# Low parts of twelve weight blocks by accumulating DMAs in a one-core hybrid layer

## The chip, the core and the metric

The kernel runs on one core of a Trainium2 chip. The core's engines work side by side, each through its own list of instructions in order: TensorE (PE, matmuls and transpositions), VectorE (DVE), ScalarE (ACT), GpSimd (POOL) and SyncE (SP, which issues transfers). The metric is the device time of one launch in microseconds. The kernel before takes 933.18 us in the median of three runs (931.96 to 933.34).

## The reference

One layer of a model in fp32 for 512 prompt rows and 64 sample rows (576 columns in all once transposed), width 1024:

```python
h = x + concat[gdn(n), diff_attention(n)] @ w_out          # n = rmsnorm(x) @ w_in, split
h = h + mem_attn(rmsnorm(h), mem_k, mem_v, w_mem_q, w_mem_o)
h = h + square(relu(rmsnorm(h) @ w_ff1)) @ w_ff2
y = rmsnorm(h)
```

The outputs are y for both groups, the new keys and values, the recurrent states and the memory keys and values. The change concerns three products with a 1024 x 1024 weight: `w_out`, `w_mem_q` and `w_mem_o`.

## The kernel before, in words

**Three products for one.** Every fp32 product is made of three fast products in the type fp32r, which rounds its operand. A value v is kept as a high part hi = round(v) and a low part lo = v - hi, and the kernel adds hi x hi, hi x lo and lo x hi in PSUM.

**A weight block** is 128 columns of a weight, all 1024 rows: a tile of 128 partitions by 8 x 128 values, 512 KB. `split_weights` makes its parts. SP loads `raw` (L569; rows of 128 values, 512 bytes); ACT casts it into the high part `wh` (L573); DVE writes the low part `wl` = raw - wh (L574). There are three buffers for `raw`, two for `wh` and two for `wl`, so a cast can start only when PE has left the high part of the block before the last one.

**A block's product.** `project` (L581) multiplies a block with the transposed activations in two halves of 256 and 320 columns, each into its own PSUM bank, over eight steps of 128 rows. In the half of 256 the two products that use `wh` are one matmul of 512 columns, followed by one of 256 with `wl`; in the half of 320 there are two with `wh` and one with `wl`. A block so has 40 matmuls. The activation's high and low parts stand in the tiles `u`.

**The stages that the change touches**, in the order of time: the output projection with eight blocks m = 0 to 7 (356.5 to 407.4 us); the memory query, four heads with two blocks each, eight blocks, with the attention of each head behind them (407.4 to 487.8 us); the memory output with eight blocks in the order m = 0, 4, 1, 5, 2, 6, 3, 7 (487.8 to 547.3 us). In the memory output `combine(m)` normalises the columns of the residual, and between the last blocks the first matmuls of the feed-forward part (FFN) are started.

**What sets the order.** The instructions are traced, and then a planner in the same file puts each engine's list into a fixed order. A `Step` holds one instruction with a modelled duration (L94 on; for a transfer a rate in bytes per ns and a lead in ns). `Arrangement.run` plays the lists out with these costs (`execute`, L392), `improve` tries priorities and keeps the order with the shortest modelled end, and `arrange` fixes that order by dependences. In this model a transfer holds its engine for 530 ns, its bytes go one after another over one wire, and a margin `SPARE` of 2500 ns is added to its landing. The order of PE's list is thus made from modelled times, while each instruction waits on the chip for its real inputs. POOL issues no transfer in this kernel; between 356 and 547 us its list holds a single operation, the power -1/2 of the query's norm (`rpow`, L618).

Of the kernel before, what the change touches and what calls it, by code (L numbers as in the profile page):

```python
# [9 lines left out]
F32 = mybir.dt.float32  # L10
F32R = mybir.dt.float32r
AF = mybir.ActivationFunctionType
ALU = mybir.AluOpType
# [3 lines left out]
P = 128  # L17
D = 1024
KT = 8
# [22 lines left out]
COLD = 9000.0  # L42
BACKLOG = 2500.0
SPARE = 2500.0
# [49 lines left out]
class Step:  # L94
# [24 lines left out]
    def cost(self):  # L119
        on_chip = [a.size for a in self.ins + self.outs if a.on_chip]  # L120
        n = max(on_chip + [1])
        wide = [a for a in self.ins if a.size > 1 or len(self.ins) == 1]
        bank = any(a.bank for a in wide)
        column = any(a.size == 1 for a in self.ins)
        if self.engine == "PE":
            x, w = self.ins
            self.passes = 2 if "32r" not in str(self.inst.ins[0].dtype) and not self.turn else 1
            self.fetch = 111.0 if self.turn else max(105.0 * w.size / 128, 55.0)
            n = x.size * self.passes
            by_size = {512: 229.0, 384: 175.0, 320: 146.5, 288: 132.5, 256: 119.0}  # L130
            single = self.passes == 1 and n > 128
            self.step = single and by_size.get(n) or max(0.42 * n + (12 if single else 4), 56.0)
            latency = {512: 400, 384: 340, 320: 310, 288: 295, 256: 281, 128: 276, 64: 222}
            self.time = latency.get(n) or (222 + 0.418 * n if n < 128 else 172 + 0.43 * n)
        elif self.is_dma:
            self.bytes = 4 * self.outs[0].size * self.outs[0].dims[0][1]
            row = 4 * min(self.ins[0].run, self.outs[0].run)
            self.rate = 270.0 if row <= 512 else 300.0 if row < 2048 else 320.0 if row < 4096 else 380.0
            if row >= 1024 and min(a.dims[0][1] for a in self.ins + self.outs if a.on_chip) <= 64:
                self.rate *= 0.6  # L140
            self.lead = 1600.0 if self.ins[0].on_chip else 1950.0
        elif self.engine == "ACT":
            self.time = (155 if bank else 190) + 0.84 * n + 100 * (len(self.ins) > 1) + 60 * (len(self.outs) > 1)
        elif self.engine == "DVE":
            if self.op == "Memset":
                self.time = 60 + 0.83 * n
            elif self.op == "Reciprocal":
                self.time = 165 + 5.4 * n
            elif self.op == "TensorScalarPtr" and len(wide) == 1:
                rate = 0.53 if not any(a.bank for a in wide) else 1.16 if n > 300 else 1.04  # L150
                self.time = 150 + rate * n + 60 * (column and n < 300)
            else:
                self.time = 145 + 1.06 * n + 62 * (column and self.op == "TensorScalarPtr")
        else:
            power = self.op == "TensorTensor" and any(a.tile.startswith("nhalf") for a in self.ins)
            by_op = dict(TensorTensor=(185, 2.2), TensorScalarPtr=(185, 2.2), TensorScalarAffineSelect=(150, 1.8))
            base, rate = (500, 140) if power and n <= 16 else by_op.get(self.op, (100, 0.85))
            self.time = base + rate * n


class Arrangement:
# [230 lines left out]
    def execute(self, s):  # L392
        at = self.start(s)
        if s.boundary:
            return at
        if s.engine == "PE":
            for i in range(s.passes):
                began, step = self.last
                slow = 2 if began < COLD else 1
                at = max(began + slow * step, max(began, 0 if i else s.ready) + slow * max(s.fetch, self.least))  # L400
                self.last, self.least = (at, s.step), 0.0
            self.least = 112.0 if s.turn else 0.0
            return at + s.time + 14
        if s.is_dma:
            self.clock[s.engine] = at + 530
            self.wire = max(at + s.lead, self.wire) + s.bytes / s.rate
            return self.wire + (SPARE if at > 2 * COLD else 0.0)
        if s.engine == "ACT":
            table = dict(Silu="Silu", Exp="Exp").get(str(getattr(s.inst, "func", "")).split(".")[-1])
            if table not in (None, self.table):  # L410
                self.table = table
                at += 1300
        self.clock[s.engine] = at + s.time - OVERLAP[s.engine]
        if s.port:
            self.held[s.engine] = at + s.time
        return at + s.time + 10
# [15 lines left out]
def hybrid_layer_kernel(  # L432
# [10 lines left out]
    V, A, G = nc.vector, nc.scalar, nc.gpsimd  # L443
# [120 lines left out]
        nc.sync.dma_start(raw, w[:, c0 : c0 + P].rearrange("(k p) n -> p k n", p=P))  # L564
        return raw

    def split_weights(w, shape):
        raw = wp.tile(shape, F32, tag="raw", name=nm("raw"), bufs=3)
        nc.sync.dma_start(raw, w.rearrange("(k p) n -> p k n", p=P))  # L569
        wh = wp.tile(shape, F32R, tag="wh", name=nm("wh"))  # L570
        wl = wp.tile(shape, F32R, tag="wl", name=nm("wl"))
        with tc.high_priority():
            A.copy(wh, raw)  # L573
            V.tensor_tensor(wl, raw, wh.bitcast(F32), ALU.subtract)  # L574
        return wh, wl

    def weights(w, c0, kt=KT):

        return split_weights(w[:, c0 : c0 + P], [P, kt, P])

    def project(w, x, evac, kt=KT, halves=HALVES, merge=True):  # L581

# [287 lines left out]
    G_Q, G_FF, G_FIN = 16, 24, 32  # L870
# [83 lines left out]
    for typ in (1, 0, 2):  # L954
# [5 lines left out]
        for h in range(H):  # L960
            m = typ * 4 + h
# [7 lines left out]
            n = SOFF + DEC  # L969
# [77 lines left out]
    with after(behind_keys[1]):  # L1047
        for lb, e in enumerate(near_):
            s = 2 << lb
# [321 lines left out]
    oa = pair(2, F32R)  # L1371
# [247 lines left out]
    for w, out in ((w_mem_k, o_mk), (w_mem_v, o_mv)):  # L1619
        dst = tokens  # L1620
        for f in range(2):
# [23 lines left out]
            if out is o_mv and f == 0:  # L1645
                ob = pair(5, F32R)
# [50 lines left out]

    hx = [pair(i, F32R) for i in (4, 3)]
    for m in range(KT):
        project(weights(w_out[0], m * P), (oa, ob), add_residual(m, True, hx, G_Q))  # L1700
    cols = norm_columns()
    accs[0] = None

# [21 lines left out]
    mo = []  # L1725
    for h in range(H):
        qh = [small("kd" if h % 2 else "aT", [P, T], dt=F32R) for i in range(2)]
        ql = cp.tile([P, 2, T], F32R, tag=f"qz{h % 2}", name=nm("ql"))
        for i in range(2):
            def split_query(b, a0, n, more=None):  # L1730
                if more is not None:
                    q = small("zr", [P, 320])[:, :n]
                    add_to(q, b, more)
                    b = q
                A.copy(qh[i][:, a0 : a0 + n], b)
                V.tensor_tensor(ql[:, i, a0 : a0 + n], b, qh[i][:, a0 : a0 + n].bitcast(F32), ALU.subtract)

            project(weights(w_mem_q[0], (2 * h + i) * P), hx, split_query)

        pT = [lows(*tags) for tags in ((("p1", "p1"), ("S", "vn")) if h % 2 else (("vb", "vb"), ("KQ", "KQ")))]  # L1740
        pS = small("an", [P, 2, DEC])
        for t, (q0, _) in enumerate(QT):
            t0, n = TT[t]
            kk, kl = (mkT, mkl) if t < 4 else (cmT, cml)
            b = bank(("gs", "g0", "g1")[t % 3])
            for i in range(2):
                m, q = 2 * h + i, slice(q0, q0 + P)
# [7 lines left out]
            p = small("p0", [P, 512])  # L1755
# [15 lines left out]
        for i in range(2):  # L1771
            b, b2 = bank(("g0", "gs")[i]), bank(("g1", "ba")[i])
            fs = slice((2 * h + i) * P, (2 * h + i + 1) * P)
            for bi in range(2):
                m = 2 * h + i
# [159 lines left out]
        halves_to(*ws[4], A22)  # L1935

    for i, m in enumerate((0, 4, 1, 5, 2, 6, 3, 7)):
        project(weights(w_mem_o[0], m * P), mo, add_residual(m, False))
        combine(m)
        if i == 3:  # L1940
            load_stage(0)
            split_first()
# [328 lines left out]
```

## Time and profile before

| | us |
|---|---|
| median of three runs | 933.18 (931.96 to 933.34) |
| profiled execution | 931.63 |
| its span in the trace | 929.9 |
| PE busy | 920.5 (99%) |
| DVE busy | 743.5 (80%) |
| ACT busy | 586.4 (63%) |
| POOL busy | 98.2 (11%) |

The span is the time from the first to the last record of the trace; 1.7 us of the execution lie outside it. In a timeline row the first number is the start in us from the span's beginning, the second the duration, then engine, line, operation, output and inputs by the program's names without their numbers, and in brackets the idle time of the engine before it and what ended that. A group of instructions has its count behind the x, then busy time and the mean in ns of one. Matmuls overlap: the time between two starts, and not the duration in the row, is what one costs PE. In the rows of stretches each engine stands with busy us and the count of instructions, then the granted clock of PE, the share of time in which the sixteen DMA engines were busy, and what they moved.

### The profile page before, as it was taken

How to read it: one execution, taken by the hardware profiler on the slowest of the kernel's cores; microseconds unless marked ns; L12 is line 12 of the kernel's file. 1: busy time of each engine (PE TensorE's matmuls, PEld its weight loads, DVE VectorE, ACT ScalarE, POOL GpSimd, SP SyncE). 2: the span in 40 equal slices, each digit the busy share in tenths (PEclk: the TensorE clock that was granted, in tenths of full speed). 3: DMA queues.
4: the chain of work that ended last, by engine and by line, in shares of the span. 5: the costliest groups of instructions: out<-in, count | busy, mean ns of one | idle time of the engine just before them, and what ended most of it. 6: DMA issues, size and time to landing. Idle time of an engine off the chain costs nothing.

```text
span 929.9 us, 17536 instructions
## 1 busy us (share of the span) xinstructions
PE 920.5 (99%) x6648; PEld 891.9 (96%) x6648; DVE 743.5 (80%) x1622; ACT 586.4 (63%) x1333; POOL 98.2 (11%) x192
## 2 busy tenths in 40 slices
PE   9999999999999999999999999999999999999997
PEld 8999999999999888999999999999999999999996
DVE  6888897887777776666567889699999588999954
ACT  6664886545566674445445567677778577877654
POOL 2452111110100000000000000021100021200001
PEclk9999999999999999999999999999999999999999
DMA  7823421127444755331212322322323222233202
GB/s 208 270 55 91 116 58 29 35 69 196 118 118 133 266 190 173 91 118 49 62 46 76 95 68 81 92 91 91 91 92 124 82 68 91 92 101 126 85 8 103
DMA packets 111727, 96.45 MB, mean 104 GB/s; under 512 B 6584, under 2 KB 98970, under 8 KB 111130
## 3 DMA queue, kind: packets, MB, share of 16 engines
q1 hardware_dynamic: 111354, 94.80, 34.5%
q8 instruction: 52, 0.85, 0.4%
q10 hardware_dynamic: 288, 0.52, 0.2%
q14 instruction: 33, 0.27, 0.1%
HBM read 80.32 MB, written 9.75 MB: 97 GB/s over the span
## 4 chain that ended last, share of the span: by engine, by line
PE 96%; issue 1%; ACT 1%; DMA 0%; DVE 0%; POOL 0%; DVEq 0%; POOLq 0%; SPq 0%
PE pr L530 61%; PE g L530 12%; PE ba L530 12%; PE gs L530 7%; PE ba L534 3%; PE g L534 2%; DMA u<-in_x_prompt_dram 0%; PE gs L534 0%; ACT u L793 0%; POOL tiny L618 0%; DVEq L2267 0%; DVE w L1807 0%; DVE raw L1902 0%; ACT w L1806 0%; POOLq L2267 0%
## 5 line engine op out<-in xcount | busy, mean ns | idle before, releaser
L530 PE MATMUL pr<-u,wh 128*128 128x320 f32 (+3 forms) x1536 | 351.5, 318 | 0.8 <-ACT u L793 0.4
L530 PEld LDWEIGHTS pr<-u,wh 128*128 128x128 f32 x1536 | 252.2, 190 | 9.8 <-ACT wh L726 0.6
L530 PE MATMUL pr<-u,wl 128*128 128x256 f32 (+2 forms) x912 | 244.9, 301 | 0.0
L530 PEld LDWEIGHTS pr<-u,wl 128*128 128x128 f32 x912 | 163.8, 189 | 1.4 <-ACT Dt L1193 0.2
L574 DVE TENSOR_TENSOR wl<-raw,wh 128x1024 fp32r<-128x1024 f32 x65 | 79.5, 1223 | 30.7 <-ACT wh L573 29.4
L573 ACT CAST wh<-raw 128x1024 fp32r<-128x1024 f32 x65 | 68.2, 1049 | 56.3 <-PE pr L530 45.6
L530 PE MATMUL pr<-x,w 128*128 128x288 f32 x432 | 66.3, 294 | 0.0
L1807 DVE TENSOR_TENSOR w<-raw,w 128x512 fp32r<-128x512 f32 x83 | 57.2, 711 | 7.2 <-PE pr L530 4.3
L530 PEld LDWEIGHTS pr<-x,w 128*128 128x128 f32 x432 | 60.3, 188 | 0.0
L530 PE MATMUL pr<-x,wl 128*128 128x288 f32 x384 | 57.5, 296 | 0.1
L530 PEld LDWEIGHTS pr<-x,wl 128*128 128x128 f32 x384 | 52.9, 188 | 0.6 <-ACT pr L2073 0.4
L530 PE MATMUL ba<-u,wl 128*128 128x288 f32 x360 | 52.7, 295 | 0.2 <-ACT gs L2009 0.2
L1806 ACT CAST w<-raw 128x512 fp32r<-128x512 f32 x83 | 49.0, 619 | 3.1 <-DVE raw L1902 1.0
L530 PEld LDWEIGHTS ba<-u,wl 128*128 128x128 f32 x360 | 49.3, 188 | 0.4 <-ACT gs L2009 0.4
L2078 DVE TENSOR_TENSOR u<-u,pr 128x288 f32<-128x288 f32 x84 | 37.5, 450 | 8.6 <-PE pr L530 7.3
L1807 DVE TENSOR_TENSOR wl<-raw,wl 128x512 fp32r<-128x512 f32 x58 | 39.1, 700 | 5.2 <-ACT wl L1806 4.5
L2076 ACT COPY u<-pr 128x288 f32<-128x288 f32 x76 | 30.2, 397 | 20.7 <-PE pr L530 20.1
L530 PE MATMUL pr<-wh,u 128*128 128x512 f32 x128 | 41.9, 400 | 0.0
L1664 DVE TENSOR_TENSOR u<-u,pr 128x256 f32<-128x256 f32 (+1 forms) x48 | 21.8, 454 | 22.8 <-PE pr L530 21.6
L2056 POOL TENSOR_TENSOR keep<-x 128x288 f32<-128x288 f32 x8 | 6.8, 847 | 309.7 <-DVE x L2030 309.7
L1806 ACT CAST wl<-raw 128x512 fp32r<-128x512 f32 x58 | 33.4, 620 | 6.4 <-DVE raw L1899 4.4
L618 POOL TENSOR_TENSOR tiny<-tiny,nhalf 128x1 f32<-128x1 f32 (+1 forms) x13 | 8.9, 694 | 206.5 <-DVE tiny L2163 98.3
(542 smaller groups left out, 2073.0 us busy)
## 6 DMA issues: line engine op xcount, KB each, us to landing
raw<-in_w_ff_dram SPq DMA_DIRECT2D x48, 512.0 KB
raw<-in_w_in_dram SPq DMA_DIRECT2D x27, 512.0 KB
raw<-in_w_ff_dram SPq DMA_DIRECT2D x32, 256.0 KB
raw<-in_w_mem_k_dram SPq DMA_DIRECT2D x8, 512.0 KB
raw<-in_w_mem_v_dram SPq DMA_DIRECT2D x8, 512.0 KB
raw<-in_w_out_dram SPq DMA_DIRECT2D x8, 512.0 KB
raw<-in_w_mem_q_dram SPq DMA_DIRECT2D x8, 512.0 KB
raw<-in_w_mem_o_dram SPq DMA_DIRECT2D x8, 512.0 KB
```

The costliest lines, as they stand in the source:

```text
L530: nc.tensor.matmul(out, lhsT, rhs, start=start, stop=stop, skip_group_check=skip_group_check)
L534: nc.tensor.transpose(out, in_, ident[:n, :n])
L573: A.copy(wh, raw)
L574: V.tensor_tensor(wl, raw, wh.bitcast(F32), ALU.subtract)
L618: G.tensor_tensor(out, in_, bc(nhalf[: in_.shape[0], 0:1], list(in_.shape)), ALU.pow)
L1664: V.tensor_tensor(hm, hm, b, ALU.add)
L1806: A.copy(hi, src)
L1807: V.tensor_tensor(lo, src, hi.bitcast(F32), ALU.subtract)
L2056: G.tensor_tensor(t, q[:, 3], q[:, 1], ALU.subtract)
L2076: A.copy(to, b[:, :n])
L2078: V.tensor_tensor(to, to, b[:, :n], ALU.add)
```

## The change

`split_weights` gets an argument `by`. With `by="add"` ACT casts the high part as before, ACT then writes its negative into `wl`, and a transfer issued by POOL adds `raw` onto it, from one on-chip tile to the other. With `by="cast"` the high part, too, is written by a transfer of POOL that casts. With `by="again"` ACT casts and negates, and four transfers of POOL add the block's rows onto `wl` straight from DRAM, two of the eight steps each. Twelve blocks take these ways: `w_out` m = 1, 3, 5, 7 the first, the second block of each head's query the second, and `w_mem_o` m = 4, 5, 6, 7 the third. The planner gets figures of its own for POOL's transfers. Lines 569 to 581 and later move by 2 to 14 in the changed kernel.

```diff
--- before.py
+++ after.py
@@ -139,6 +139,8 @@
             if row >= 1024 and min(a.dims[0][1] for a in self.ins + self.outs if a.on_chip) <= 64:
                 self.rate *= 0.6
             self.lead = 1600.0 if self.ins[0].on_chip else 1950.0
+            if self.engine == "POOL":
+                self.rate, self.lead = 250.0, 2000.0
         elif self.engine == "ACT":
             self.time = (155 if bank else 190) + 0.84 * n + 100 * (len(self.ins) > 1) + 60 * (len(self.outs) > 1)
         elif self.engine == "DVE":
@@ -402,9 +404,9 @@
             self.least = 112.0 if s.turn else 0.0
             return at + s.time + 14
         if s.is_dma:
-            self.clock[s.engine] = at + 530
+            self.clock[s.engine] = at + (1000 if s.engine == "POOL" else 530)
             self.wire = max(at + s.lead, self.wire) + s.bytes / s.rate
-            return self.wire + (SPARE if at > 2 * COLD else 0.0)
+            return self.wire + (SPARE if at > 2 * COLD and s.engine != "POOL" else 0.0)
         if s.engine == "ACT":
             table = dict(Silu="Silu", Exp="Exp").get(str(getattr(s.inst, "func", "")).split(".")[-1])
             if table not in (None, self.table):
@@ -564,19 +566,31 @@
         nc.sync.dma_start(raw, w[:, c0 : c0 + P].rearrange("(k p) n -> p k n", p=P))
         return raw
 
-    def split_weights(w, shape):
+    def split_weights(w, shape, by=None):
         raw = wp.tile(shape, F32, tag="raw", name=nm("raw"), bufs=3)
         nc.sync.dma_start(raw, w.rearrange("(k p) n -> p k n", p=P))
         wh = wp.tile(shape, F32R, tag="wh", name=nm("wh"))
         wl = wp.tile(shape, F32R, tag="wl", name=nm("wl"))
         with tc.high_priority():
-            A.copy(wh, raw)
-            V.tensor_tensor(wl, raw, wh.bitcast(F32), ALU.subtract)
+            if by == "cast":
+                G.dma_start(wh, raw)
+            else:
+                A.copy(wh, raw)
+            if by is None:
+                V.tensor_tensor(wl, raw, wh.bitcast(F32), ALU.subtract)
+            else:
+                A.activation(wl, wh.bitcast(F32), AF.Identity, scale=-1.0)
+                if by == "again":
+                    for k in range(0, 8, 2):
+                        src = w[k * P : (k + 2) * P, :].rearrange("(k p) n -> p k n", p=P)
+                        G.dma_start(wl[:, k : k + 2], src, accum_op=ALU.add)
+                else:
+                    G.dma_start(wl, raw, accum_op=ALU.add)
         return wh, wl
 
-    def weights(w, c0, kt=KT):
-
-        return split_weights(w[:, c0 : c0 + P], [P, kt, P])
+    def weights(w, c0, kt=KT, by=None):
+
+        return split_weights(w[:, c0 : c0 + P], [P, kt, P], by)
 
     def project(w, x, evac, kt=KT, halves=HALVES, merge=True):
 
@@ -1697,7 +1711,7 @@
 
     hx = [pair(i, F32R) for i in (4, 3)]
     for m in range(KT):
-        project(weights(w_out[0], m * P), (oa, ob), add_residual(m, True, hx, G_Q))
+        project(weights(w_out[0], m * P, by="add" if m % 2 else None), (oa, ob), add_residual(m, True, hx, G_Q))
     cols = norm_columns()
     accs[0] = None
 
@@ -1735,7 +1749,7 @@
                 A.copy(qh[i][:, a0 : a0 + n], b)
                 V.tensor_tensor(ql[:, i, a0 : a0 + n], b, qh[i][:, a0 : a0 + n].bitcast(F32), ALU.subtract)
 
-            project(weights(w_mem_q[0], (2 * h + i) * P), hx, split_query)
+            project(weights(w_mem_q[0], (2 * h + i) * P, by="cast" if i else None), hx, split_query)
 
         pT = [lows(*tags) for tags in ((("p1", "p1"), ("S", "vn")) if h % 2 else (("vb", "vb"), ("KQ", "KQ")))]
         pS = small("an", [P, 2, DEC])
@@ -1935,7 +1949,7 @@
         halves_to(*ws[4], A22)
 
     for i, m in enumerate((0, 4, 1, 5, 2, 6, 3, 7)):
-        project(weights(w_mem_o[0], m * P), mo, add_residual(m, False))
+        project(weights(w_mem_o[0], m * P, by="again" if m > 3 else None), mo, add_residual(m, False))
         combine(m)
         if i == 3:
             load_stage(0)
```

The planner makes new lists from this. PE's list up to about 290 us and after about 557 us is the same. In the names below the first number of a tile counts all tiles in the order of tracing; `x2` behind a row stands for two like it.

POOL, around the output projection and the memory query. Before:

```order
L1563 TENSOR_SCALAR ta_574_3988<-ta_574_3988 128x5
L618 TENSOR_TENSOR ta_575_3989<-ta_574_3988,nhalf_86 128x5
L618 TENSOR_TENSOR tiny_746_5021<-tiny_745_5020,nhalf_86 128x5
L2056 TENSOR_TENSOR keep_1090_7435<-x_1035_6951 128x288
L2057 TENSOR_TENSOR x_1035_6951<-x_1035_6951 128x288
```

POOL, the same place in the changed kernel:

```order
L632 TENSOR_TENSOR ta_575_3989<-ta_574_3988,nhalf_86 128x5
L588 DMA wl_696_4594<-raw_694_4591 128x1024
L588 DMA wl_710_4717<-raw_708_4714 128x1024
L588 DMA wl_724_4840<-raw_722_4837 128x1024
L588 DMA wl_738_4963<-raw_736_4960 128x1024
L576 DMA wh_769_5138<-raw_768_5136 128x1024
L632 TENSOR_TENSOR tiny_746_5025<-tiny_745_5024,nhalf_86 128x5
L588 DMA wl_770_5139<-raw_768_5136 128x1024
L576 DMA wh_814_5388<-raw_813_5386 128x1024
```

The adds of m = 1, 3, 5 and 7 stand one behind the other; the second query block's casting transfer (L576) and its add (L588) have the power operation of the norm between them.

PE, output projection, where the block m = 1 (`wh_695`, `wl_696`) begins. Before:

```order
L530 MATMUL pr_693_4562<-u_671_4438,wl_691_4536 128x320 x2
L530 MATMUL pr_693_4562<-u_671_4438,wh_690_4535 128x320 x2
L530 MATMUL pr_697_4597<-u_322_2489,wh_695_4593 128x512
L530 MATMUL pr_697_4597<-u_322_2489,wl_696_4594 128x256
...
L530 MATMUL pr_697_4597<-u_671_4438,wl_696_4594 128x256 x2
L530 MATMUL pr_697_4597<-u_671_4438,wh_695_4593 128x512
L530 MATMUL pr_699_4621<-u_322_2489,wh_695_4593 128x320 x2
```

PE, the same place in the changed kernel (`wh_702` is the high part of m = 2):

```order
L532 MATMUL pr_693_4562<-u_671_4438,wh_690_4535 128x320 x2
L532 MATMUL pr_697_4598<-u_322_2489,wh_695_4593 128x512
L532 MATMUL pr_699_4622<-u_322_2489,wh_695_4593 128x320 x2
L532 MATMUL pr_704_4659<-u_322_2489,wh_702_4655 128x512
L532 MATMUL pr_697_4598<-u_322_2489,wl_696_4594 128x256
L532 MATMUL pr_697_4598<-u_322_2489,wh_695_4593 128x512
```

Three matmuls that need no low part moved ahead of the first that needs m = 1's, the last of them on the high part of m = 2. At m = 3 two and at m = 5 and m = 7 one matmul of 320 columns moved ahead in the same way.

PE, memory query, where the second block (`wh_769`, `wl_770`) begins. Before:

```order
L530 MATMUL pr_767_5105<-u_688_4532,wl_764_5080 128x320 x2
L530 MATMUL pr_767_5105<-u_688_4532,wh_763_5079 128x320 x2
L530 MATMUL pr_771_5138<-u_687_4531,wh_769_5134 128x512
L530 MATMUL pr_771_5138<-u_687_4531,wl_770_5135 128x256
...
L534 MATMUL ba_755_5046<-ident_81,u_749_5035 128x128 x4
L534 MATMUL ba_756_5053<-ident_81,u_749_5035 128x128 x4
```

PE, the same place in the changed kernel:

```order
L532 MATMUL pr_771_5143<-u_687_4531,wh_769_5138 128x512
L532 MATMUL pr_773_5165<-u_687_4531,wh_769_5138 128x320 x2
L532 MATMUL gs_779_5197<-u_614_4156,aT_759_5078 128x256
...
L532 MATMUL g1_76<-u_614_4156,ql_761_5080 128x256
L532 MATMUL pr_810_5337<-u_687_4531,wh_808_5333 128x512
L532 MATMUL pr_771_5143<-u_687_4531,wl_770_5139 128x256
```

Two matmuls of the other half, nine score matmuls of the first head (into `gs`, `g0`, `g1`, three each; they use the first query block's result) and the first matmul of the third block now stand ahead of the first that uses the second block's low part. In the memory output the same was done at m = 6: there eighteen matmuls of the first FFN stage stand ahead of the first use of its low part, where seven stood before.

## The prediction

> **What bounds the kernel now.** I read the page first: its span, busy times and chain of waits.
>
> ```profile
> span 929.9 us, 17536 instructions
> PE 920.5 (99%) x6648; PEld 891.9 (96%) x6648; DVE 743.5 (80%) x1622; ACT 586.4 (63%) x1333; POOL 98.2 (11%) x192
> ...
> PE 96%; issue 1%; ACT 1%; DMA 0%; DVE 0%; POOL 0%; DVEq 0%; POOLq 0%; SPq 0%
> ```
>
> TensorE is busy for 99% of the span and makes up 96% of the chain; VectorE, which the change relieves, is 0% of it. Then the waits of PE from 340 us to the end, and the busy times of the first two stages the change touches (output projection, memory query), with two short stretches of dense transfers below them:
>
> ```profile
> PE ba L530 <- ACT gs L2009: 0.2, 1, 0.2
> ...
> core 0: us, PE busy (x) PEld busy (x) DVE busy (x) ACT busy (x) POOL busy (x), PEclk, DMA share, GB/s
> 356.50:407.40 50.90, 50.90 (x323) 47.92 (x322) 33.63 (x62) 22.23 (x41) 0.00 (x0) 1.00 0.36 105
> 407.40:487.80 80.40, 80.40 (x541) 75.34 (x540) 49.33 (x146) 38.83 (x105) 1.17 (x1) 1.00 0.23 66
> ...
> 339.40:340.80 1.40, 1.40 (x10) 1.20 (x8) 1.40 (x3) 0.80 (x1) 0.00 (x0) 1.00 0.81 271
> 385.45:387.81 2.36, 2.36 (x19) 2.36 (x18) 1.69 (x4) 0.82 (x2) 0.00 (x0) 1.00 0.80 222
> ```
>
> In 590 us PE waits once for data, 0.2 us. In both stages it is busy for the whole stretch at full clock while DVE works for 33.63 of 50.90 and 49.33 of 80.40 us. So the change has next to nothing to win here: **0.2 us of waits is the cap** on what relief of another engine can give, unless PE's own list gets shorter. Its matmuls are the same ones, and by the new order its transpositions stand in as many groups as before. The question is what the new, longer way to a weight block's low part makes PE wait.
>
> **The change part by part.**
>
> *What is removed.* Twelve subtractions on DVE, and four casts on ACT:
>
> ```profile
> L574 DVE TENSOR_TENSOR wl<-raw,wh 128x1024 fp32r<-128x1024 f32 x23 | 28.1, 1222 | 18.6 <-ACT wh L573 18.6
> L573 ACT CAST wh<-raw 128x1024 fp32r<-128x1024 f32 x23 | 24.1, 1049 | 30.2 <-PE pr L530 20.0 <-issue 9.2 <-DMA raw<-in_w_mem_o_dram 1.0
> L530 PEld LDWEIGHTS pr<-u,wl 128*128 128x128 f32 x384 | 71.1, 188 | 1.0
> ```
>
> 12 x 1.222 = 14.7 us of DVE and 4 x 1.05 = 4.2 us of ACT, all beside a busy PE: worth 0. I grant -0.2 us, the one wait. *What is added* to ACT: twelve negations, taken at the cast's 1.05 us because they have its shape, 12.6 us; ACT's 22.23 of 50.90 us leaves room for them.
>
> *What decides: X, the time from issue on POOL to landing of one 512 KB add.* The profile shows no transfer issued by POOL, so X has to be bounded:
>
> ```profile
> q1 hardware_dynamic: 111354, 94.80, 34.5%
> ...
> q10 hardware_dynamic: 288, 0.52, 0.2%
> ...
> 527.31 0.37 SPq L569 DMA_DIRECT2D raw<-in_w_mem_o_dram  x1
> ...
> 531.46 1.06 ACT L573 CAST wh<-raw 128x1024 fp32r<-128x1024 f32 x1 [0.96 <-DMA raw<-in_w_mem_o_dram]
> ...
> 412.30 1.17 POOL L618 TENSOR_TENSOR tiny<-tiny,nhalf 128x5 f32<-128x5 f32 x1 [78.10 <-DMA u<-in_cache_mem_k_dram]
> ```
>
> An ordinary block of the same size is issued at 527.31 and releases the cast that waits for it at 531.46: 4.15 us. At the 222 GB/s of such loads the bytes take 2.36 us. The add moves 4 KB rows rather than 512 B rows, so I give it the fastest stretch above, 271 GB/s: 1.93 us, 0.43 less. Its issue costs POOL some time: the nearest row is POOL's small operation, 1.17 us against SP's 0.37, 0.80 more. X = 4.15 - 0.43 + 0.80 = **4.5 us**, if reading the destination overlaps reading the source. Upper end: the destination is a second pass, 4.5 + 1.93 = 6.4. Lower end: SP's cheap issue and the bytes at 271/0.81 = 335 GB/s (all sixteen engines busy), 1.6 us: 4.15 - 2.36 + 1.6 = 3.4.
>
> [...]
>
> *Output projection, blocks m = 1, 3, 5, 7.* Rows for m = 1 (and the cast of m = 2), then 3 and 7:
>
> ```profile
> 357.19 1.05 ACT L573 CAST wh<-raw 128x1024 fp32r<-128x1024 f32 x1
> 363.04 1.05 ACT L573 CAST wh<-raw 128x1024 fp32r<-128x1024 f32 x1 [1.30 <-PE pr L530]
> 362.55 0.69 PE L530 MATMUL pr<-u,wh 128*128 128x320 f32 x3
> 363.07 0.28 PE L530 MATMUL pr<-u,wl 128*128 128x256 f32 x1
> 363.19 0.40 PE L530 MATMUL pr<-u,wh 128*128 128x512 f32 x1
> 363.43 0.28 PE L530 MATMUL pr<-u,wl 128*128 128x256 f32 x1
> ...
> 369.39 1.05 ACT L573 CAST wh<-raw 128x1024 fp32r<-128x1024 f32 x1 [1.79 <-PE pr L530]
> 375.76 0.28 PE L530 MATMUL pr<-u,wl 128*128 128x256 f32 x1
> ...
> 394.77 1.05 ACT L573 CAST wh<-raw 128x1024 fp32r<-128x1024 f32 x1 [1.79 <-PE pr L530]
> 401.15 0.28 PE L530 MATMUL pr<-u,wl 128*128 128x256 f32 x1
> ```
>
> PE's steps, start to start: 0.12 us for 256 columns (363.07 to 363.19), 0.24 for 512, about 0.147 for 320 (0.52 us from 362.55 to 363.07 is two of these and one of 512). For m = 1 the new order pulls two 320s and **the first matmul of m = 2** ahead of m = 1's low part. PE reaches that one at 363.07 + 0.29 = 363.37, but its weights are cast only from 363.04 to 364.09, once m = 0 has left the buffer; with 0.19 us for the weight load (188 ns above) it starts at 364.28. **+0.9 us**, whatever X is. The low part of m = 1 itself is wanted at 364.28 + 0.24 - 0.19 = 364.33; its negation ends at 357.19 + 2.10 = 359.29, so it is late only from X = 5.0.
>
> For m = 3 the negation ends at 371.49; two 320s are pulled ahead, and the low part is wanted at 375.76 + 0.29 - 0.19 = 375.86: room for 4.4, short by 0.1. For m = 7 one 320 is pulled ahead: ready to add at 396.87, wanted at 401.15 + 0.15 - 0.19 = 401.11: room for 4.24, short by 0.26; m = 5 has the same distances. Together **+0.6 us**. PE waits in order here, so nothing later in its list can fill the gap.
>
> *Memory query.* Rows for the second block, and for the fourth, which the sixth and eighth are like:
>
> ```profile
> 407.47 1.05 ACT L573 CAST wh<-raw 128x1024 fp32r<-128x1024 f32 x1 [1.80 <-PE pr L530]
> 409.33 1.22 DVE L574 TENSOR_TENSOR wl<-raw,wh 128x1024 fp32r<-128x1024 f32 x1
> 413.84 0.69 PE L530 MATMUL pr<-u,wh 128*128 128x320 f32 x3
> 414.36 0.28 PE L530 MATMUL pr<-u,wl 128*128 128x256 f32 x1
> ...
> 422.74 1.05 ACT L573 CAST wh<-raw 128x1024 fp32r<-128x1024 f32 x1
> 437.25 0.28 PE L530 MATMUL pr<-u,wl 128*128 128x256 f32 x1
> ```
>
> The fourth has 14.5 us from the free buffer to its low part, against 2X + 1.05 = 10.05, so only the second matters.
>
> Its buffer comes free at 407.47. The casting transfer lands X later, 411.97; the negation ends 413.02. POOL's power operation (412.30 to 413.47, quoted above; up to 1.22 earlier now that DVE's subtraction at 409.33 is gone) stands ahead of the add in POOL's queue, so the add is issued between 413.02 and 413.47 and lands at 417.5 to 418.0. PE takes one matmul of 512, two of 320, nine score matmuls of 256 and one of 512 first (the last pair of lists ahead of this): 414.36 + 0.29 + 9 x 0.12 + 0.24 = 415.97, weights wanted at 415.78. Late by 1.7 to 2.2: **+2.0 us**. Queued behind it are PE's own next matmuls and transpositions only, which all shift.
>
> *Memory output, blocks 4 to 7.* The adds come in quarters straight from DRAM, each with its own wait, and the low part is used a quarter at a time; I cost these at nothing, since eighteen first-FFN matmuls were put ahead of block 6's low part. Those need block 2's normalised columns:
>
> ```profile
> 526.04 0.68 PE L530 MATMUL pr<-u,wh 128*128 128x512 f32 x3
> 526.06 1.22 DVE L574 TENSOR_TENSOR wl<-raw,wh 128x1024 fp32r<-128x1024 f32 x1
> 527.20 0.48 DVE L1664 TENSOR_TENSOR u<-u,pr 128x320 f32<-128x320 f32 x1
> 527.71 0.78 ACT L1814 ACTIVATE x<-u,gcol 128x576 f32<-128x576 f32 x1 [2.21 <-DVE u L1664]
> 528.52 0.43 ACT L1806 CAST B<-x 128x288 fp32r<-128x288 f32 x1
> 528.99 0.46 DVE L1807 TENSOR_TENSOR B<-x,B 128x288 fp32r<-128x288 f32 x1
> ```
>
> With the subtraction at 526.06 gone, that chain starts 0.9 us earlier and its two results are there at about 528.05 and 528.55. PE comes to the first matmul on them at 526.04 + 0.53 + 12 x 0.133 (a step of 288) = 528.2, to the last of its two halves 0.8 later: **+0.4 us**, between 0 and 0.8.
>
> *Sum at X = 4.5:* 0.9 + 0.6 + 2.0 + 0.4 - 0.2 = **+3.7 us**. The profiled execution took 931.63 us (span 929.9 and 1.7 around it), so 935.3; it lies 1.55 us below the median 933.18, to which a median compares: **936.9 us**. By the same steps X = 3.4 gives +1.6 (the low parts of 3, 5, 7 in time, the query block 0.5), X = 5.1 gives +6.5, X = 6.4 gives +14.3.
>
> **Rivals.**
>
> *R1, the adds land in time (not slower).* If X is 3.6 or less, only the pulled matmul (0.9), the query block (0.5) and the tail remain: +1.6 us at X = 3.4, 934.8, less if the tail costs nothing: 934.2. That is within 0.2% (1.87 us), about what a measurement of this kernel can tell from no change. For it: 335 GB/s is what the wire would give, and 23 to 36% of it is in use in the two stages. Against: the 4.15 us of an ordinary load.
>
> *R2, POOL is held while it issues.* If POOL cannot write a transfer's descriptors while DVE works, each add waits for one DVE operation, 1.22 us by L574: X = 5.7. Then 0.9 + 0.7 (m = 1), 1.3, 2 x 1.46, query 407.47 + 2X + 1.05 = 419.92 against 415.78, 4.1, and 0.4 - 0.2: +10.1 us, **943.3**. For it: DVE is busy for two thirds of the projection. Against: POOL's power operations run at 1.17 us beside a busy DVE here. The same price comes from a destination read that is half serial (X = 5.5).
>
> [...]
>
> *R3, relief pays (faster).* 14.7 us of DVE work gone lets the planner regroup. Bounded by 0.2 us of waits on PE until the order itself gets shorter by 1.9 us, which as many transposition groups as before speak against: 932.9.
>
> **How the numbers follow.** Forecast (X from 3.6 to 5.1) 0.42, of it 0.05 under the bound; R1 0.30, of it 0.03 faster through a tail that gains; R2 0.20; R3 0.08, of it 0.05 faster by more than the bound. Faster 0.08, same 0.05 + 0.27 + 0.03 = 0.35, slower 0.37 + 0.20 = 0.57. The likeliest case has 935 to 939.7; the range reaches to R3's point and R2's: 932.8 to 944.
>
> **What would show it.** PE's waits must name a transfer into wl: none or under 0.2 us at m = 1, 3, about 0.3 at 5 and 7, 2.0 at the second query block, and a wait for ACT's cast of 0.9 at about 363.4. POOL's issues give X: between its row and the matmul it releases. A span of 933.6 with PE's busy time unchanged bears out the sum; PE waits of several us in the other query blocks or at the quarters of 5 and 7 would make it wrong, as would a gap before 290 us, where PE's order is the same.

## The result: 5.3% slower, and the profile after

The changed kernel takes 982.09 us in the median of four runs (981.46 to 983.22), the kernel before 932.97 us beside it: a ratio of 1.053, 95% interval 1.0511 to 1.0548. The forecast had the right sign and a thirteenth of the size: +3.7 us against +49.

Span, busy times, clock row, the new transfer queue and the chain, from the page of the changed kernel, and the landing times of POOL's transfers (KB each, then the median in us from issue to landing), from its list of transfers:

```profile
span 980.0 us, 17590 instructions
PE 937.2 (96%) x6648; PEld 901.0 (92%) x6648; DVE 732.5 (75%) x1610; ACT 593.3 (61%) x1341; POOL 126.1 (13%) x220
...
PEclk9999999999999999999998888999999999999998
...
q0 software_dynamic: 6080, 8.39, 4.6%
...
PE 83%; issue 6%; DMA 4%; ACT 3%; POOL 2%; DVE 1%; SPq 0%; DVEq 0%; POOLq 0%; ACTq 0%
...
wl<-raw POOLq DMA_DIRECT2D x8, 512.0 KB, 4.6
...
wh<-raw POOLq DMA_DIRECT2D x4, 512.0 KB, 2.9
wl<-in_w_mem_o_dram POOLq DMA_DIRECT2D x16, 128.0 KB, 3.6
```

DVE's busy time falls by 11.0 us, and it buys nothing. PE has the same 6648 matmuls but is busy 16.7 us longer (937.2 against 920.5), and idle 33.4 us longer (42.8 against 9.4): the two make up the 50.1 us of span. The longer busy time stands under the digits 8 of the clock row. The idle time is in PE's waits from 290 us to the end:

```profile
PE pr L532 <- DMA wl<-in_w_mem_o_dram: 27.1, 10, 4.5
PE pr L532 <- DMA wl<-raw: 4.4, 5, 2.9
PE gs L532 <- ACT aT L1749: 0.6, 1, 0.6
PE pr L532 <- ACT wh L578: 0.6, 1, 0.6
PE pr L532 <- DMA wh<-raw: 0.2, 1, 0.2
PE ba L532 <- ACT gs L2023: 0.2, 1, 0.2
```

27.1 of 33 us are waits for the quarters of the memory output, the part that the forecast cost at nothing. By stage, the busy rows of the changed kernel (projection, query, memory output), and behind them the memory output of the kernel before:

```profile
357.44:411.75 54.31, 52.14 (x323) 47.83 (x322) 28.82 (x58) 26.44 (x45) 3.73 (x4) 1.00 0.54 137
411.75:499.49 87.74, 83.95 (x541) 76.72 (x539) 47.44 (x142) 39.18 (x106) 6.88 (x9) 0.98 0.41 109
499.49:597.38 97.89, 70.64 (x382) 62.95 (x380) 44.51 (x103) 34.91 (x67) 19.36 (x16) 0.84 0.36 76
```

```profile
487.78:547.28 59.50, 59.50 (x381) 55.62 (x380) 48.63 (x107) 31.76 (x63) 0.00 (x0) 1.00 0.30 89
```

In this table the same is done for every kernel that ran: a stage goes from its first matmul on a high weight part to that of the next, the memory output to its last. The last column is the time ratio to the kernel before, with its interval.

| kernel | projection | query | memory output | ratio |
|---|---|---|---|---|
| before | 50.91 | 80.37 | 59.50 | 1 |
| changed | 54.31 (+3.4) | 87.74 (+7.4) | 97.89 (+38.4) | 1.053 (1.0511 to 1.0548) |
| 1: POOL's descriptor area doubled | 54.25 | 88.91 | 68.03 | 1.0222 (1.0207 to 1.0237) |
| 2: memory output as before | 54.45 | 87.74 | 59.64 | 1.0132 (1.0117 to 1.0147) |
| 3: quarters from on chip | 54.60 | 88.86 | 66.42 | 1.0194 (1.0174 to 1.0214) |
| 4: query of heads 1 to 3 alone | 50.90 | 81.44 | 59.51 | 1.0019 (1.0009 to 1.0029) |
| 5: query of head 0 alone | 50.91 | 87.06 | 59.53 | 1.0070 (1.0055 to 1.0085) |
| 6: the same, only the add a transfer | 50.90 | 80.67 | 59.47 | 1.0006 (0.9997 to 1.0016) |
| 7: as 5, with needless matmuls | 50.90 | 85.55 | 59.51 | 1.0058 (1.0040 to 1.0076) |
| 8: one add in place of four quarters | 54.45 | 88.53 | 69.09 | 1.0224 (1.0198 to 1.0250) |

Runs 3 and 8 have two executions each, the others four or more. Ahead of these stages the profiles differ by up to 1.8 us, with nothing changed there. Runs 9 and 10, below, move work across the edges of the stages and are left out here.

### The profile page after: what moved, and what is told of

Read it like the earlier page. It is cut to its first block, busy times and chain, and to the rows that moved or that the text cites. A ratio compares the mean times of both kernels' runs of the same rounds, so it can differ in the third digit from the quotient of the medians.

```text
span 980.0 us, 17590 instructions
## 1 busy us (share of the span) xinstructions
PE 937.2 (96%) x6648; PEld 901.0 (92%) x6648; DVE 732.5 (75%) x1610; ACT 593.3 (61%) x1341; POOL 126.1 (13%) x220
## 3 DMA queue, kind: packets, MB, share of 16 engines
q0 software_dynamic: 6080, 8.39, 4.6%
## 4 chain that ended last, share of the span: by engine, by line
PE 83%; issue 6%; DMA 4%; ACT 3%; POOL 2%; DVE 1%; SPq 0%; DVEq 0%; POOLq 0%; ACTq 0%
PE pr L532 51%; PE ba L532 11%; PE g L532 10%; PE gs L532 6%; PE ba L536 2%; DMA wl<-raw 2%; PE g L536 2%; DMA wl<-in_w_mem_o_dram 1%; POOL wl L586 1%; ACT wl L582 1%; ACT wh L578 1%; DMA u<-in_x_prompt_dram 1%; POOL tiny L632 0%; PE gs L536 0%; DVE accq L2196 0%
## 5 line engine op out<-in xcount | busy, mean ns | idle before, releaser
L532 PE MATMUL pr<-u,wh 128*128 128x320 f32 (+3 forms) x1536 | 359.0, 323 | 1.9 <-ACT wh L578 0.6
L532 PE MATMUL pr<-u,wl 128*128 128x256 f32 (+2 forms) x912 | 249.7, 306 | 31.5 <-DMA wl<-in_w_mem_o_dram 27.1
L532 PEld LDWEIGHTS pr<-u,wh 128*128 128x128 f32 x1536 | 257.6, 194 | 11.6 <-ACT wh L578 0.9
L532 PEld LDWEIGHTS pr<-u,wl 128*128 128x128 f32 x912 | 167.3, 193 | 38.1 <-DMA wl<-in_w_mem_o_dram 30.5
L578 ACT CAST wh<-raw 128x1024 fp32r<-128x1024 f32 x61 | 63.9, 1048 | 73.8 <-PE pr L532 71.6
L580 DVE TENSOR_TENSOR wl<-raw,wh 128x1024 fp32r<-128x1024 f32 x53 | 64.9, 1224 | 24.3 <-ACT wh L578 22.3
L1820 ACT CAST wl<-raw 128x512 fp32r<-128x512 f32 x58 | 33.4, 620 | 16.3 <-DVE raw L1913 14.1
L586 POOL DMA_DIRECT2D wl<-in_w_mem_o_dram x16 | 19.4, 1210 | 86.7 <-ACT wl L582 48.0
```

The source lines that it names most:

```text
L532: nc.tensor.matmul(out, lhsT, rhs, start=start, stop=stop, skip_group_check=skip_group_check)
L586: G.dma_start(wl[:, k : k + 2], src, accum_op=ALU.add)
L1820: A.copy(hi, src)
```

## The experiments

**The quarters.** POOL's list in the changed kernel, the four quarters of block m = 4 (start, duration of the issue, and the idle time before it with what ended it):

```profile
500.47 1.25 POOL L586 DMA_DIRECT2D wl<-in_w_mem_o_dram  x1 [17.41 <-ACT wl L582]
504.42 1.21 POOL L586 DMA_DIRECT2D wl<-in_w_mem_o_dram  x1 [2.70 <-issue]
508.28 1.21 POOL L586 DMA_DIRECT2D wl<-in_w_mem_o_dram  x1 [2.65 <-issue]
513.57 1.21 POOL L586 DMA_DIRECT2D wl<-in_w_mem_o_dram  x1 [4.07 <-issue]
```

An issue takes 1.21 us, as the forecast had it (1.17). But between two of them POOL stands still for 2.65 us and more, and "issue" says that it waits for nothing that the profile shows: the program has no semaphore there. The transfer records show that the first packet of the second quarter (506.35) comes 2.6 us after the end of the first quarter's last (503.76), and that POOL's second issue starts 0.7 us after that end (504.42). Either POOL has no room for a second quarter's descriptors, or it never starts one transfer ahead of the end of another.

Run 1 changes only the room (and, to make it, the count of some small buffers; its lists are those of the changed kernel on every engine):

```diff
-    def tiny(shape, tag="tiny", bufs=16):
+    def tiny(shape, tag="tiny", bufs=12):
...
-    nc = _bacc.Bacc("TRN2", target_bir_lowering=False, num_devices=1, dynamic_dma_scratch_size=1024)
+    nc = _bacc.Bacc("TRN2", target_bir_lowering=False, num_devices=1, dynamic_dma_scratch_size=2048)
```

> The changed kernel with POOL's descriptor area doubled from 1024 to 2048 bytes (the small scratch tiles go from 16 buffers to 12 to make the room; every engine's list is the same as in the changed kernel). In the changed kernel the four quarters of a block in the memory output are issued 3.8 to 3.9 us apart, though none of the last three waits for a semaphore. Theory A, the area is too small for two quarters at once (256 rows of 512 bytes each): with twice the room at least two quarters go out 1.2 us apart, PE's waits on the quarters fall from 27.1 us to under 14, and the time from 982 to below 965. Theory B, POOL starts a transfer only when the one before has ended, whatever the area: 3.8 to 3.9 us stay, and 982 within 1.5 us.

Measured: 952.73 us. POOL's rows for the same block, and PE's wait on the quarters:

```profile
501.01 3.70 POOL L586 DMA_DIRECT2D wl<-in_w_mem_o_dram  x3 [17.34 <-ACT wl L582]
504.88 1.21 POOL L586 DMA_DIRECT2D wl<-in_w_mem_o_dram  x1 [0.17 <-issue]
...
PE pr L532 <- DMA wl<-in_w_mem_o_dram: 4.7, 6, 1.8
```

Three quarters now go out one behind the other in 3.70 us, and only the fourth has to wait. The waits fall from 27.1 to 4.7 us, the stage from 97.89 to 68.03. So it is room: theory A. About 28 us of the 49 (21.0 are left, beside this run's own runs of before) hang on one number at the bottom of the file, which neither the forecast nor the planner's model looked at.

Run 3 leaves the area as it was and halves the rows of a quarter instead, by reading them from the tile on chip:

```diff
-                        src = w[k * P : (k + 2) * P, :].rearrange("(k p) n -> p k n", p=P)
+                        src = raw[:, k : k + 2]
```

> The changed kernel, but the four quarters of a memory-output block are added from the on-chip raw tile, 128 rows of 1 KB each instead of 256 rows of 512 bytes from DRAM: half the rows. Theory A (room for descriptors): two or three quarters go out 1 to 1.2 us apart, waits on the quarters under 14 us, time below 965. Theory B (one transfer after the other): still 3.3 to 3.8 us apart, time 972 to 982.

Measured: 949.85 us. Again three go out together with 1024 bytes:

```profile
500.91 2.66 POOL L586 DMA_DIRECT2D wl<-raw  x3 [17.34 <-ACT wl L582]
503.94 0.86 POOL L586 DMA_DIRECT2D wl<-raw  x1 [0.36 <-issue]
```

The two runs bracket the room, if it is counted in packets. By the transfer records a quarter from DRAM has 272 packets, and one from on chip has 144 by the count of run 3's queue (4032 = 28 x 144, where the changed kernel's 6080 are 12 x 144 + 16 x 272): 17 and 9 for each of sixteen engines, if they are spread evenly. From these counts I estimate the room: with 1024 bytes three of 9 fit and two of 17 don't, between 27 and 33 packets for each engine; with 2048 three of 17 fit and four don't, between 51 and 67.

Run 8 replaces the quarters by one on-chip add of a whole block, which leaves nothing to queue:

```diff
-        project(weights(w_mem_o[0], m * P, by="again" if m > 3 else None), mo, add_residual(m, False))
+        project(weights(w_mem_o[0], m * P, by="add" if m > 3 else None), mo, add_residual(m, False))
```

> The changed kernel, but the four blocks of the memory output take the first way (one 512 KB add each from the on-chip raw tile) in place of four quarters from DRAM. Theory A (four transfers with room for one at a time are the loss): the stage of the memory output falls from 97.9 us to below 66, the time to 943 to 951. Rival (any accumulating transfer is too late there): stage above 75 us.

Measured: 953.36 us, with a stage of 69.09 us, both above what theory A expected, though far from its rival. One of the four blocks makes most of what is left: its add is issued at 540.24, its first packet comes only at 543.26 (1.4 us after the issue at the other three), while SP's loads of two more weight blocks (issued at 538.73 and 539.37, their packets until 543.94) keep the transfer engines busy (285 GB/s from 540 to 544 us), and PE then waits for 2.3 us.

**Whether a better order hides it.** Run 9 keeps all edits and tells the planner what the chip showed:

```diff
-                self.rate, self.lead = 250.0, 2000.0
+                self.rate, self.lead = 190.0, 2400.0
...
+            if s.engine == "POOL":
+                self.clock["POOL"] = self.wire
             return self.wire + (SPARE if at > 2 * COLD and s.engine != "POOL" else 0.0)
```

> The changed kernel as it is, but the planner is told what the chip showed: 190 bytes per ns and a lead of 2400 ns for POOL's transfers, and that POOL's next instruction starts only when its transfer has landed. Theory (capacity): a block's buffer for the low part comes free one block ahead, 6.35 us, while cast, negation and four quarters one after the other need 1.05 + 1.05 + 15.5 = 17.6 us; no order has that much other work to put in between, so the stage of the memory output stays above 85 us (97.9 in the changed kernel) and the time above 968. Rival (price): the loss comes from an order made with wrong prices, and with right ones the stage falls below 70 us.

Measured: 963.83 us (ratio 1.0345, 1.0328 to 1.0362); the memory output takes 84.6 us, with more of the FFN's matmuls inside it. My bounds of 85 and 968 were too high by a little: the planner finds work for 17 of the 49 us, with FFN matmuls put between the quarters. PE's waits on the quarters fall to 11.1 us, and 32 us of loss remain. Prices alone don't mend it, and capacity alone doesn't explain it.

**The two other stages.** Run 2 takes the edit of the memory output back (`by=None` in its line).

> The changed kernel without its edit of the memory output (all eight blocks by the old way); the output projection and the memory query as changed. By the stage times of the two traces the projection gave away 3.4 us and the query stage 7.4: 10.8, 943.8 us. If the blind forecast's terms for these two stages were right (0.9 + 0.6 + 2.0 = 3.5), 936.5.

Measured: 944.19 us, +12.4 beside its own runs of before; in its profile the two stages are 10.9 us longer. So the forecast was three times too low here too, without the quarters. Runs 4 and 5 split the query stage:

```diff
-            project(weights(w_mem_q[0], (2 * h + i) * P, by="cast" if i else None), hx, split_query)
+            project(weights(w_mem_q[0], (2 * h + i) * P, by="cast" if i and h else None), hx, split_query)
```

is run 4, and the same with `by="cast" if i and not h else None` is run 5; in both, the other two stages are as before.

> Only the second query block of heads 1, 2 and 3 takes the new way (casting transfer, negation, add); everything else as before. Those three have 14.5 us from the free buffer to the low part, and need 2 x 4.5 + 1.05 = 10.1. Theory of the forecast: DVE relief is worth nothing and nothing waits: 932.9 within 0.9 us. Rival (relief pays): faster by more than 1.9 us. Rival (even these wait): slower by more than 1.9 us.

> Only the second query block of head 0 takes the new way; everything else as before. In the changed kernel its casting transfer was issued 0.3 us after SP's load of the memory keys (1 MB) and landed 6.4 us after its issue, where the forecast had 4.5; ACT's negation waits for it in ACT's list and holds the conversion of the first query behind it. Theory: this one block makes the whole loss of the query stage beside the order's own 1.07 us (seen where only heads 1 to 3 were changed): the stage is 6 to 7.4 us longer than before, the kernel slower by 6 to 7.4 us. Rival, the loss of that stage is spread over all four heads: under 4 us.

Run 4: 933.37 us, 1.6 above its own runs of before: more than the 0.9 of the theory, less than the 1.9 of its rivals. No wait of PE is added (its only wait is the 0.2 us of before), DVE has three subtractions fewer, and the stage is 1.07 us longer with PE busy for 81.34 of its 81.44 us. It has the same matmuls at a clock of 1.00, so I put the 1.07 us down to the order that the planner made, which no run tests. Relief of DVE pays nothing even where it costs no wait. Run 5: 938.81 us, the stage +6.7: head 0's block is the loss. What happens at it in the changed kernel, on SP, POOL, ACT and PE:

```profile
411.81 0.37 SPq L1724 DMA_DIRECT2D u<-in_cache_mem_k_dram  x1
412.08 0.56 POOL L576 DMA_DIRECT2D wh<-raw  x1 [10.27 <-PE pr L532]
418.92 1.06 ACT L582 ACTIVATE wl<-wh 128x1024 fp32r<-128x1024 f32 x1 [3.36 <-DMA wh<-raw]
420.33 0.92 POOL L588 DMA_DIRECT2D wl<-raw  x1 [3.96 <-ACT aT L1749]
...
420.32 0.39 PE L532 MATMUL gs<-u,aT 128*128 128x256 f32 x1 [0.65 <-ACT aT L1749]
...
424.96 0.39 PE L532 MATMUL pr<-u,wl 128*128 128x256 f32 x1 [2.85 <-DMA wl<-raw]
```

SP issues a load of 1 MB, POOL 0.27 us later its casting transfer, and that lands behind it: the negation starts 6.84 us after the issue, where such a transfer takes 2.9 us in the other heads. By the transfer records the load's packets run from 412.83 to 417.22 and the cast's first comes at 416.81, against 1.1 us after the issue in the other heads. It isn't that the first such transfer is slow: in run 4 the first is that of head 1, and its packets begin 1.4 us after the issue (422.87 and 424.23). ACT stands for 3.36 us with the negation at the head of its list, and the first query's conversion (`aT`) behind it, for which PE then waits. Run 6 lets ACT cast this block:

```diff
-            project(weights(w_mem_q[0], (2 * h + i) * P, by="cast" if i and not h else None), hx, split_query)
+            project(weights(w_mem_q[0], (2 * h + i) * P, by="add" if i and not h else None), hx, split_query)
```

> As the run before, but ACT casts the block's high part, and only the low part's add is a transfer: the negation no longer waits for a transfer behind SP's load, and ACT's list is not held. Theory (the cast behind the load is the cause): no wait of more than 1 us, stage longer by 0 to 2 us. Rival (the add alone is late enough): 3 us or more of waiting at this block, stage longer by over 4 us.

Measured: 932.55 us, 1.0006 (0.9997 to 1.0016); no wait of PE is left but the old one, and the stage is 0.30 us longer. So the loss comes from the casting transfer, which stands behind the load, and not from the add.

**The clock.** In run 5 PE idles 3.9 us of the stage's 6.7. The rest is in its busy time. Run 7 keeps PE busy during the wait:

```diff
+                    for _ in range(again if a0 == k == i == 0 else 0):
+                        mm(out, w[part][:, k, :], moving, start=True, stop=True)
                     mm(out, w[part][:, k, :], moving, start=k == i == 0, stop=last and i == len(order) - 1)
```

(`again`, a new argument of `project`, is 18 at this block and 0 elsewhere.)

> As the kernel in which only head 0's second block takes the new way, but the block's first high-part matmul is done 19 times instead of once (18 needless ones, 18 x 0.233 = 4.2 us of work for PE; the last one counts). They keep PE busy while the low part is on its way. Theory C, half of what a long wait costs is TensorE's clock, granted at half for some 4 us after it (0.65 in the 4 us after the 3 us wait of the changed kernel): with PE kept busy the clock stays at 1.00 and the stage is 0.5 to 2 us shorter than without the needless work. Rival, the lost time is the wait alone: the stage is as long or longer, by up to 2 us, and the clock row shows no difference.

The stage in 4 us pieces around the block; run 5, then run 7 (behind the busy times the granted clock, then transfer share and GB/s):

```profile
416.00:420.00 4.00, 2.51 (x13) 1.72 (x13) 2.05 (x3) 2.52 (x4) 0.94 (x1) 1.00 0.34 66
420.00:424.00 4.00, 2.06 (x10) 2.05 (x11) 0.34 (x1) 0.69 (x2) 0.00 (x0) 0.80 0.50 106
424.00:428.00 4.00, 4.00 (x23) 3.49 (x22) 1.87 (x4) 1.63 (x3) 0.00 (x0) 0.78 0.81 222
```

```profile
416.00:420.00 4.00, 4.00 (x23) 3.41 (x22) 2.50 (x4) 2.89 (x6) 0.94 (x1) 1.00 0.52 98
420.00:424.00 4.00, 3.92 (x26) 3.25 (x25) 2.22 (x4) 1.18 (x3) 0.00 (x0) 1.00 0.54 138
424.00:428.00 4.00, 4.00 (x30) 3.96 (x29) 0.85 (x2) 0.78 (x2) 0.00 (x0) 1.00 0.63 161
```

With 18 matmuls more the stage is 1.5 us shorter (85.55 against 87.06), and the clock stays at 1.00: theory C. The run times, 937.79 and 938.81 us, point the same way but their ranges overlap; the clock row and the stage decide, with one trace of each kernel. In run 5 the busy time of the stage is 83.18 us, 2.8 over that of before. The clock stood at 0.50 for 3.4 us of it (422.39 to 425.80), which is worth 1.7 at most; the rest is the new order and the dearer first matmul behind a wait (0.23 us to the next start at 421.94, against the 0.12 of such matmuls without a wait), which I can't tell apart.

**All blocks the gentle way.** Run 10 takes ACT's cast and one on-chip add for all twelve, with the planner's price of run 9 but without its line on POOL's clock.

> The changed kernel with its twelve low parts all by ACT's cast, ACT's negation and one on-chip add of 512 KB (no casting transfer, no quarters), and the planner told 190 bytes per ns and a lead of 2400 ns. Theory: waits of up to 1 us each remain, none long enough for the clock: projection 0.5 to 2 us longer, query 0 to 1.5, memory output 0 to 4, together 933.5 to 939; never faster than before, since PE has nothing to win. Rival (relief of DVE pays once the waits are gone): faster than before by over 1.9 us.

Measured: 941.42 us (1.0102, 1.0087 to 1.0117), above the expected span; no relief shows. Its waits:

```profile
PE pr L532 <- ACT wh L578: 3.1, 5, 0.6
PE pr L532 <- DVE wl L580: 1.1, 1, 1.1
PE ba L532 <- ACT B L1820: 0.6, 1, 0.6
PE pr L532 <- DMA wl<-raw: 0.6, 1, 0.6
```

The waits for low parts are nearly gone; in their place PE waits five times for a high part (L578), which ACT's cast has not written by then. I take this to be the planner pulling the next block's first matmul ahead of the low part; no run tests it. These rows make 5.4 of the 9.6 us. In all three stages the granted clock is 1.00. The rest I have not taken apart.

## Why the prediction was wrong, step by step

**What bounds the kernel: right.** PE sets the end, relief of DVE is worth nothing (runs 4, 6, 10: ratios 1.0019, 1.0006, 1.0102), and the sign follows from that.

**X: right, by luck.** Chosen 4.5 us for one 512 KB add; the landing column says 4.6. The reason given was wrong by halves: the packets of an add take 2.77 us, where the sum had 1.93, and those of the casting transfer, with as many bytes, 1.45. The 1.3 us between them would fit a second pass for the destination's reading, which the sum kept for its upper end; no run tests that. All the rest takes 1.8 us (4.6 - 2.77), where the sum had 2.6 (4.5 - 1.93). Two errors cancelled.

**Output projection, 0.9 + 0.6: measured 3.4.** The places were right, each a little dearer:

```profile
365.08 0.49 PE L532 MATMUL pr<-u,wh 128*128 128x512 f32 x1 [0.61 <-ACT wh L578]
365.92 0.38 PE L532 MATMUL pr<-u,wl 128*128 128x256 f32 x1 [0.35 <-DMA wl<-raw]
...
374.46 0.87 POOL L588 DMA_DIRECT2D wl<-raw  x1 [12.74 <-ACT wl L582]
379.07 0.39 PE L532 MATMUL pr<-u,wl 128*128 128x256 f32 x1 [0.47 <-DMA wl<-raw]
```

The pulled matmul of m = 2 waited for its cast, 0.78 us by the steps against 0.9. But m = 1's low part, "late only from X = 5.0", was late as well (0.6 us): the add of that block landed after 5.3 us, beside a load and a store of SP that were still moving when it was issued (392 GB/s from 360 to 361 us). At m = 3, 5 and 7 the sum lacked the 0.3 us from the negation's end to POOL's issue (374.15 to 374.46) and about 0.1 us behind each wait, where the first matmul of 256 columns took 0.22 us to the next start (365.92 to 366.14, 379.07 to 379.29) against 0.12.

**Memory query, 2.0: measured 7.4.** The block and the chain were named. Failed: "The casting transfer lands X later, 411.97", which left out the 1 MB load that SP issues at the same moment (in the kernel before, too, it stands at 407.46); and "Queued behind it are PE's own next matmuls and transpositions only", which left out ACT, whose list the negation held. Waits 3.7, clock 1.7 at most (3.4 us at 0.50), order 1.1 (run 4); the rest, about 0.9, is not taken apart.

**Memory output, 0 + 0.4: measured 38.4.** This is the step that lost the forecast: "The adds come in quarters ... I cost these at nothing". The only reason given was eighteen FFN matmuls, and they stand ahead of one block of the four. Nothing was set against them: neither when POOL could issue four transfers one behind the other, nor when each was wanted. They went out 3.8 us apart or more, mostly 3.9. A block then needs 1.05 + 1.05 + 15.3 us (three distances of 3.9 and a landing of 3.6) from a free buffer to its last quarter, and the buffers of `wh` and `wl` come free one block, 6.35 us, ahead. The two bounds for X did not reach this case, because they bound one transfer and not four behind each other on one queue. The prediction's own sign of being wrong, PE waits of several us at the quarters, is what came. The 0.4 us of the tail didn't come in the changed kernel: no wait of PE names that chain.

**What no step had: the clock.** Of the 38.4 us, 27.1 are waits and 11.1 are a longer busy time (70.64 against 59.50). The stretches of the memory output in which the granted clock was halved:

```profile
517.37:520.78 3.41, 3.41 (x14) 3.31 (x14) 1.58 (x4) 0.00 (x0) 0.00 (x0) 0.50 0.28 101
534.44:544.68 10.24, 4.93 (x16) 4.23 (x17) 1.99 (x6) 0.00 (x1) 1.32 (x2) 0.50 0.36 70
565.16:571.98 6.82, 3.99 (x14) 3.56 (x14) 0.00 (x0) 0.00 (x0) 1.92 (x2) 0.50 0.32 38
585.64:595.88 10.24, 6.09 (x20) 5.39 (x21) 2.81 (x5) 0.28 (x1) 1.21 (x1) 0.50 0.21 26
```

PE around one wait, and then around another one, with two half-microsecond stretches behind it:

```profile
517.11 0.59 PE L532 MATMUL pr<-u,wl 128*128 128x256 f32 x2 [2.15 <-DMA wl<-in_w_mem_o_dram]
...
520.05 0.47 PE L532 MATMUL pr<-u,wl 128*128 128x320 f32 x1
...
521.27 0.31 PE L532 MATMUL pr<-u,wl 128*128 128x320 f32 x1
...
533.07 0.39 PE L532 MATMUL pr<-u,wl 128*128 128x256 f32 x1 [2.88 <-DMA wl<-in_w_mem_o_dram]
...
533.50:534.00 0.50, 0.50 (x3) 0.19 (x1) 0.00 (x0) 0.00 (x0) 0.50 (x1) 1.00 0.02 7
534.50:535.00 0.50, 0.00 (x0) 0.00 (x0) 0.00 (x0) 0.00 (x0) 0.05 (x1) 0.50 0.85 250
```

In these four stretches PE is busy for 18.42 us at half clock: an estimate of 9.2 us lost, most of the 11.1. The same matmul takes 0.47 us at 520.05 and 0.31 us at 521.27. After the waits of 0.3 to 0.6 us in the projection the clock stayed at 1.00 (its stage row).

It was not the length of a single wait that decided. After the wait of 2.15 us the clock fell 0.3 us behind PE's next start; after that of 2.88 us PE went on at 1.00, and the clock fell within the next wait. These stretches last 3.41 us or two or three times that, and in the traces the granted clock changed only on a grid of 3.41 us. Divided along this grid, the twelve traces (before, changed, runs 1 to 10) show this: a piece at full clock in which PE idled for less than 1.3 us was never followed by one at half clock, a piece with more than 1.9 us always was, and between the two it went both ways (the least idle time ahead of a drop is 1.39 us, the most without one 1.83). So three short waits within one piece did it too (0.85, 0.65 and 0.61 us in run 3, half clock from 546.40 on), while one of 1.50 us in run 1 did not. At the first stretch above PE idled for 2.15 us of the 3.41 us ahead, and that was enough for the drop; from 517.37 to 520.78, at half clock, it was busy throughout, and then the clock was back at 1.00.

**The rivals.** R1 (in time) and R3 (relief pays) did not come. R2 put its price on POOL being held by DVE, and no run shows that: POOL's issues in the changed kernel took 0.55 to 1.25 us, and an add landed after 4.6 us, where R2 had 5.7. POOL was held, but by its own descriptors: doubling the area let three quarters out back to back in 3.70 us beside nearly the same DVE work (733.2 us busy against 732.5).

## What to carry to other kernels

Before a transfer is put on a queue that the profile has not shown, ask three things beside its duration: how many of them that queue can hold at once, what else is issued in the microsecond ahead of it, and what stands behind the instruction that waits for it on its own engine. Count the way from a freed buffer to the value against the time by which the buffer comes free ahead of its use: here 1.05 + 1.05 + 0.3 + 4.6 = 7.0 us against 6.35 for blocks that follow one another, so that even one add per block could not be hidden there. And idle time of TensorE that came close together was paid for again in these traces: more than 1.9 us of it within one piece of 3.41 us halved the clock for the next.

## What the runs showed of the hardware that I had not expected

- POOL held its next transfer, with no wait in the program, until there was room for its descriptors: 3.9 us from issue to issue with quarters of 272 packets and 1024 bytes, 1.2 us for the first three with 2048.
- An accumulating transfer took nearly twice the wire time of a casting one of the same size: 2.77 against 1.45 us for the packets of 512 KB, and 4.6 against 2.9 us from issue to landing.
- TensorE's granted clock went by pieces of 3.41 us: it was halved after each with more than 1.9 us of idle time, in one wait or in several, and 18 needless matmuls in place of a wait made a stage shorter by 1.5 us.
- A POOL transfer issued 0.27 us behind a 1 MB load of SP had its last packet 6.4 us after its issue, against 2.6 us in the other heads; its first packet started when the load's last ones did (416.81, the load's until 417.22).
